# A hybrid decoder step: the cross-attention samples' chain in 20 steps per head, and the GLA gate logits as two rounded products

## The chip, the cores and the metric

The kernel runs on one core of one Trainium2 chip. The metric is the device time of one execution in microseconds (us). Five engines work side by side, each through its own queue in order: TensorE (PE in the profile, its weight loads PEld), VectorE (DVE), ScalarE (ACT), GpSimd (POOL) and SyncE (SP), which here does nothing but issue loads.

## The reference

One layer of a hybrid trunk for a prompt of 1024 tokens and a group of 8 single-token samples. One input projection feeds three branches; each is projected, gated and summed, and one output projection follows. Cut to what the change touches:

```
def mixer_layer(x, mem_k, mem_v, S0, pool_hist, pos0, ...):
    proj = rmsnorm(x) @ w_in
    q, k, v, gla_g, a_lr, u, pool_g, xq, xg, merge = split(proj)
    # A: gated linear attention, 4 heads, key 128, value 256, gate rank 16
    z = a_lr @ w_a2 + b_a                       # the gate logits
    log_a = log_sigmoid(z) / 16
    o, S = gla_chunked(q, k, v, log_a, S0)
    # C: cross attention, 4 heads of 256, over 256 memory rows
    s = einsum('bthd,bmhd->bhtm', xq, mem_k) * 256 ** -0.5
    c = einsum('bhtm,bmhd->bthd', softmax(s), mem_v)
```

The prompt attends to a memory that the kernel projects itself, the same for all 1024 tokens. Each of the 8 samples has memory keys and values of its own (cache_mem_k, cache_mem_v: 256 rows of 256 per head and sample), so its scores are 256 dot products of 256 numbers per head.

## The kernel before

**The projection is the beat.** Products in f32 accuracy are made of rounded halves (type fp32r): each operand is split into hi and lo, and mm3 (L242 to L244) sums hi·hi, hi·lo and lo·hi. The input projection goes by a seven-product scheme (run_product) over 40 column pairs. A product has two stretches of 12 matmuls of 258 columns. Behind each stretch fill() takes the next pieces of a second stream, mix(), by costs that the pieces yield; so between two stretches of the projection stand one or two small pieces of attention. One stretch is called a slot below. mix() runs cross_steps() and then gla_steps(); the first fills about 120 to 370 us of the span, the second the part up to some 700 us.

**What sets the order.** The rows of TensorE and SyncE stand in the order in which the program is written (manual_schedule). VectorE, ScalarE and GpSimd get theirs from a scheduler, which ranks rows by its own estimate. All five then work in order: a row that waits holds everything behind it on its engine. Tiles come from rings: R (14 buffers of 128x512), V (4, loads of keys, values and broadcast queries), W (halves of the projection's weights), and PZ (2 PSUM buffers, for all of attention). A tile can be written only when the last reader of the tile that had its buffer is done.

**Cross attention of the prompt** goes in 16 units s (4 heads by 4 groups of 256 queries). scores(s) (cross_scores, 12 matmuls, L242 to L244) takes keys mkTh and mkTl, and queries xqsh and xq, which cross_queries (L697) splits from a loaded xq on ACT (L226) and DVE (L227). The softmax is on DVE and ACT (nm L709, p L75). weights(s) transposes p (L724) and splits the result into pTh (ACT L223) and pTl (DVE L224). values(s) multiplies them by the memory's values; ACT writes xo (L736), and POOL stores it (L737, mixsc). memory(s) transposes the keys of the next head.

**The samples' chain** (cross_sample, L754) is run one step at a time between these pieces. cross_rows (L744) transposes the scaled queries of the 8 samples to rows, and POOL stores them (L752, tile xqs). fetch(b2) issues, for two samples, two loads of keys (kc, 256 KB each) and one load qb of the two query rows (L767), which repeats each over 128 partitions. DVE multiplies and sums (L777, 4 rows for two samples), into the scores sc. After four pairs: transposes of sc (L791), softmax (nm L793, ps L75, L797, L798), transposes of ps (L803), a copy to pm (L804); then twice four loads vc and 16 matmuls with pm (L817), read by ACT into cs (L819); then transposes of cs (L827). kc, qb and vc share ring V of 4 buffers: a pair's kc and qb take three.

**The gate logits.** w_a2 stays resident as w2, f32, in four copies of its 16 rows at partitions 0, 32, 64 and 96; the projection leaves a_lr as four partial sums at the same partitions, stored in al_scr. gla_load (L896) loads alc, 256 tokens of it, and gla_gates (L904) makes the logits of a head in one f32 matmul (L907), 16 blocks in all; gla_sample does the same for the 8 samples (L1012, 4 blocks).

## Time and profile before

| | us |
|---|---|
| median of 3 runs (lowest, highest) | 1442.38 (1441.68, 1443.36) |
| the profiled execution: its own time | 1445.01 |
| the profiled execution: its span | 1443.3 |
| TensorE busy (share) | 1417.4 (98%) |
| VectorE busy | 916.2 (63%) |
| ScalarE busy | 679.0 (47%) |
| GpSimd busy | 222.1 (15%) |

The profiler records one execution. Its span runs from the first to the last instruction; what lies around it is 1.7 us. An engine's busy time is the time in which it had an instruction at work; matmuls overlap, so a busy TensorE is not one at its peak. The views read below list what an engine waited for and which tile or transfer ended the wait, the busy time of all engines in chosen stretches with the clock granted to TensorE (1.00 is 2.4 GHz, 0.50 is 1.2 GHz), and timelines of single instructions.

### The profile page before, as it was taken

The numbers are of one execution on the slowest core, as the hardware profiler recorded it, in microseconds if no ns is written. First come the engines' busy times: TensorE is split into PE (matmuls) and PEld (weight loads), VectorE is DVE, ScalarE is ACT, GpSimd is POOL, SyncE is SP. The second block draws the span as 40 slices with busy tenths as digits, with TensorE's granted clock in tenths as the row PEclk, the third lists the DMA queues.
The fourth block names the chain that finished last, engine by engine and source line by source line (L and its number), as shares of the span: only waits on it lengthen the run. The fifth ranks groups of instructions, "written<-read, shape, count | busy, mean of one in ns | idle before, by whom it ended". The sixth has DMA issues, their size and how long they took to land.

```text
span 1443.3 us, 28179 instructions
## 1 busy us (share of the span) xinstructions
PE 1417.4 (98%) x10689; PEld 1356.1 (94%) x10689; DVE 916.2 (63%) x2123; ACT 679.0 (47%) x1575; POOL 222.1 (15%) x401
## 2 busy tenths in 40 slices
PE   8999999999999999999999999999999999999998
PEld 6899999989899999999999999999999999999876
DVE  6954756666687777767766778785672434554436
ACT  6743544443465666656654445444472432233212
POOL 3211111124342121212221111111010000000000
PEclk9999999999999999999999999999999999999999
DMA  9355665656656363554654455454694777632633
GB/s 329 125 165 169 217 218 187 207 175 165 198 155 193 115 192 129 182 176 126 187 167 150 149 188 170 159 184 163 204 298 134 234 257 249 234 104 79 224 118 116
DMA packets 183507, 259.42 MB, mean 180 GB/s; under 512 B 22204, under 2 KB 132564, under 8 KB 183364
## 3 DMA queue, kind: packets, MB, share of 16 engines
q1 hardware_dynamic: 159900, 183.87, 41.5%
q0 software_dynamic: 23328, 73.56, 14.7%
q8 instruction: 84, 1.38, 0.4%
q14 instruction: 51, 0.42, 0.1%
q10 hardware_dynamic: 144, 0.20, 0.0%
HBM read 180.47 MB, written 77.56 MB: 179 GB/s over the span
## 4 chain that ended last, share of the span: by engine, by line
PE 88%; DMA 5%; DVE 5%; issue 1%; ACT 1%; SPq 0%; POOL 0%; DVEq 0%; ACTq 0%; POOLq 0%
PE px L242 25%; PE px L243 25%; PE px L244 25%; DMA qb<-xqs 3%; PE pz L244 2%; PE pz L243 2%; PE pz L242 2%; DMA raw<-in_w_in_dram 1%; DVE kc L777 1%; PE pz L963 1%; PE pz L404 1%; PE pz L944 1%; PE pz L817 1%; PE pz L946 1%; PE pz L907 0%
## 5 line engine op out<-in xcount | busy, mean ns | idle before, releaser
L244 PE MATMUL px<-bh,wbl 128*128 128x384 f32 (+1 forms) x576 | 184.1, 320 | 0.0
L243 PE MATMUL px<-bl,wbh 128*128 128x384 f32 (+1 forms) x576 | 184.1, 320 | 0.0
L242 PE MATMUL px<-bh,wbh 128*128 128x384 f32 (+1 forms) x576 | 183.7, 319 | 0.0
L554 ACT ACTIVATE r<-px 128x258 f32<-128x258 f32 x240 | 89.9, 375 | 47.4 <-PE px L244 46.9
L242 PEld LDWEIGHTS px<-bh,wbh 128*128 128x128 f32 x576 | 108.3, 188 | 0.0
L243 PEld LDWEIGHTS px<-bl,wbh 128*128 128x128 f32 x576 | 108.2, 188 | 0.0
L244 PEld LDWEIGHTS px<-bh,wbl 128*128 128x128 f32 x576 | 108.2, 188 | 0.0
L242 PE MATMUL px<-ot,s1h 128*128 128x258 f32 x320 | 94.1, 294 | 0.0
L242 PE MATMUL px<-o,a12h 128*128 128x258 f32 x320 | 93.4, 292 | 0.0
L242 PE MATMUL px<-ot,s3h 128*128 128x258 f32 x320 | 93.2, 291 | 0.0
L242 PE MATMUL px<-o,s4h 128*128 128x258 f32 x320 | 93.0, 291 | 0.2 <-DVE c L636 0.2
L242 PE MATMUL px<-o,a11h 128*128 128x258 f32 x320 | 92.8, 290 | 0.0
L242 PE MATMUL px<-ot,a22h 128*128 128x258 f32 x320 | 92.6, 289 | 0.0
L242 PE MATMUL px<-ot,s2h 128*128 128x258 f32 x320 | 92.2, 288 | 0.0
L243 PE MATMUL px<-o,a11h 128*128 128x258 f32 x320 | 91.1, 285 | 0.3 <-DVE o L224 0.3
L243 PE MATMUL px<-o,a12h 128*128 128x258 f32 x320 | 91.1, 285 | 0.0
L244 PE MATMUL px<-o,a12l 128*128 128x258 f32 x320 | 91.0, 284 | 0.0
L244 PE MATMUL px<-ot,s1l 128*128 128x258 f32 x320 | 90.9, 284 | 0.0
L243 PE MATMUL px<-ot,s1h 128*128 128x258 f32 x320 | 90.8, 284 | 0.0
L244 PE MATMUL px<-o,a11l 128*128 128x258 f32 x320 | 90.6, 283 | 0.0
L243 PE MATMUL px<-ot,s2h 128*128 128x258 f32 x320 | 90.1, 281 | 0.5 <-DVE ot L224 0.5
L243 PE MATMUL px<-ot,a22h 128*128 128x258 f32 x320 | 90.5, 283 | 0.0
(471 smaller groups left out, 4634.3 us busy)
## 6 DMA issues: line engine op xcount, KB each, us to landing
raw<-in_w_in_dram SPq DMA_DIRECT2D x80, 512.0 KB, 4.0
msc<-c POOLq DMA_DIRECT2D x24, 516.0 KB, 4.8
brsc<-c POOLq DMA_DIRECT2D x24, 516.0 KB, 3.7
sig<-msc SPq DMA_DIRECT2D x24, 516.0 KB, 6.0
brr<-brsc SPq DMA_DIRECT2D x48, 256.0 KB, 5.2
wbr<-in_w_branch_dram SPq DMA_DIRECT2D x24, 512.0 KB, 5.5
acc<-sig POOLq DMA_DIRECT2D x16, 516.0 KB, 5.2
acc<-acc SPq DMA_DIRECT2D x16, 516.0 KB, 7.0
```

The lines of the kernel that those rows point to most:

```text
L242: nc.tensor.matmul(out, lhsT=lh, rhs=rh, start=start, stop=False, skip_group_check=more)
L243: nc.tensor.matmul(out, lhsT=lh, rhs=rl, start=False, stop=False, skip_group_check=more)
L244: nc.tensor.matmul(out, lhsT=ll, rhs=rh, start=False, stop=stop, skip_group_check=more)
L404: nc.tensor.matmul(t[:, :DV], lhsT=memT[k // 2][:, k % 2, a * P:(a + 1) * P], rhs=raw[k // 2][:, k % 2], start=k == 0, stop=k == NK - 1)
L554: nc.scalar.activation(r, acc[c][:, :QT], AF.Copy)
L777: nc.vector.tensor_tensor_reduce(kc[:, a, :], kc[:, a, :], qb[:, bb, :], scale=1.0, scalar=0.0, op0=ALU.mult, op1=ALU.add, accum_out=sc[:, ...
L817: nc.tensor.matmul(t[32 * j:32 * j + 32, :DV], lhsT=pm[:, a, 4 * i + j, :], rhs=vc[j][:, a, :], start=a == 0, stop=a == 1)
L944: nc.tensor.matmul(t[0:64, 0:P], lhsT=ki[:, 0:64], rhs=qi, start=True, stop=True)
L946: nc.tensor.transpose(t[:, P:2 * P], kt, ident)
L963: nc.tensor.matmul(to, lhsT=kiqi[:, 1, cs], rhs=st, start=False, stop=True)
```

## The change

**The samples' chain.** Its steps are cut and spread anew, 20 per head instead of 16. One sample's sums are a step of their own. The loads of keys and query rows move to cross_keys, which is called two pairs ahead: for pairs 0 and 1 at the end of the head before, for pairs 2 and 3 at samples 2 and 4. The query rows leave ring V: each sample has a tile qb of its own, in buffers of the tags alc and st, which GLA uses later, and one load of 128 KB; so 32 loads instead of 16. Ring V now holds two pairs of kc. cross_scaled and cross_rows of the next head move behind the softmax and between the two blocks of sample values. There are more steps between the softmax and the transposes of ps, and the loads of vc are issued ahead of these. At the beginning the queries are loaded before the memory's transposes, a step lies between these and the split of the queries, and the rows of head 0 are made right before the first scores.

**The gate logits.** w2 is no longer resident. gate_weights (at unit 6) loads w_a2 eight times into 128 partitions, splits it on ACT and DVE, and stores both halves by eight POOL stores in w2_scr. gate_inputs (at units 7 and 8) loads the stored a_lr, whose 16 rows now stand twice in each group of 32 partitions (wa is copied once more by POOL at the start), and makes of it a stack in which one copy holds the rounded part and the other the rest: one ACT row and two POOL rows of 128x512, and a POOL store. gla_gates then takes two fp32r matmuls, with the halves of w_a2, on the stacked tile. gla_load has one more small load per head.

```
-    w2 = cp.tile([P, 512], F32, name="w2")
-    nc.vector.memset(w2, 0.0)
+    gm = cp.tile([P, 4], F32, name="gm")
+    nc.vector.tensor_reduce(gm[:, 0:2], ident.rearrange("p (j e r) -> p e j r", j=4, e=2), axis=AX.XY, op=ALU.add)
+    nc.vector.tensor_tensor(gm[:, 2:3], gm[:, 0:1], gm[:, 1:2], op=ALU.subtract)
+    second_copy, copy_sign = gm[:, 1:2], gm[:, 2:3]
...
     wa = R([NK, 32], name="wa")
-    nc.vector.memset(wa, 0.0)
 
     def small_loads():
         nc.gpsimd.dma_start(out=wa[:, :, :GATE], in_=w_in[:, O_A:O_A + GATE].rearrange("(k p) n -> p k n", p=P))
-        for j in range(4):
-            nc.gpsimd.dma_start(out=w2[32 * j:32 * j + GATE], in_=w_a2)
+        nc.gpsimd.tensor_copy(wa[:, :, GATE:], wa[:, :, :GATE])
...
+    def cross_keys(h, b2):
+        kc = [loaded(ck[2 * b2 + bb, :, h, :].rearrange("(a p) d -> p a d", p=P), [2, DV], "kc", V) for bb in range(2)]
+        qb = [wk.tile([P, DV], F32, tag=t, name="qb", bufs=2) for t in ("alc", "st")]
+        for bb in range(2):
+            nc.sync.dma_start(out=qb[bb], in_=xq_scr[h][2 * b2 + bb].partition_broadcast(P))
+        cross["kc", h, b2] = kc, qb
+
     def cross_sample(h):
 
-        if h == 0:
-            cross_scaled(0)
-            cross_rows(0)
-            yield 1.2
-            yield 0.5
-            yield 0.5
         sc = wk.tile([P, 16], F32, tag="sc", name="sc", bufs=2)
-
-        def fetch(b2):
-            kc = [loaded(ck[2 * b2 + bb, :, h, :].rearrange("(a p) d -> p a d", p=P), [2, DV], "kc", V) for bb in range(2)]
-            qb = V([2, DV], name="qb")
-            nc.sync.dma_start(out=qb, in_=xq_scr[h][2 * b2:2 * b2 + 2].partition_broadcast(P))
-            return kc, qb
-
-        kcs, qb = fetch(0)
-        yield 0.5
-        yield 0.5
-        for b2 in range(4):
-            for bb in range(2):
-                b, kc = 2 * b2 + bb, kcs[bb]
-                for a in range(2):
-                    nc.vector.tensor_tensor_reduce(kc[:, a, :], kc[:, a, :], qb[:, bb, :],
-                                                   scale=1.0, scalar=0.0, op0=ALU.mult, op1=ALU.add,
-                                                   accum_out=sc[:, a * NS + b:a * NS + b + 1])
-            if b2 == 2 and h + 1 < NH:
-                cross_scaled(h + 1)
-            if b2 < 3:
-                kcs, qb = fetch(b2 + 1)
-                yield 1.2
-            elif h + 1 < NH:
-                cross_rows(h + 1)
-            yield 1
+        for b in range(NS):
+            kcs, qb = cross["kc", h, b // 2]
+            kc = kcs[b % 2]
+            for a in range(2):
+                nc.vector.tensor_tensor_reduce(kc[:, a, :], kc[:, a, :], qb[b % 2],
+                                               scale=1.0, scalar=0.0, op0=ALU.mult, op1=ALU.add,
+                                               accum_out=sc[:, a * NS + b:a * NS + b + 1])
+            if b in (2, 4):
+                cross_keys(h, b // 2 + 1)
+            yield 0.7
...
         nc.vector.tensor_scalar(p, p, sm, None, op0=ALU.mult)
-        yield 1.2
-        yield 0.5
+
+        def own_values(i):
+            return [loaded(cv[4 * i + j, :, h, :].rearrange("(a p) d -> p a d", p=P), [2, DV], "vc", V) for j in range(4)]
+
+        vc = own_values(0)
+        if h + 1 < NH:
+            cross_scaled(h + 1)
+        yield 1.5
         t = PZ()
         for a in range(2):
             nc.tensor.transpose(t[:, a * NS:(a + 1) * NS], p[:, a * P:(a + 1) * P], ident[:NS, :NS])
         nc.vector.tensor_copy(pm[:, :, :, 0], t[:, :2 * NS].rearrange("p (a b) -> p a b", a=2))
-
-        def own_values(i):
-            return [loaded(cv[4 * i + j, :, h, :].rearrange("(a p) d -> p a d", p=P), [2, DV], "vc", V) for j in range(4)]
-
-        vc = own_values(0)
         yield 1.2
         yield 0.5
         cs = R([2, DV], name="cs")
@@ -817,10 +807,20 @@
                     nc.tensor.matmul(t[32 * j:32 * j + 32, :DV], lhsT=pm[:, a, 4 * i + j, :], rhs=vc[j][:, a, :],
                                      start=a == 0, stop=a == 1)
             nc.scalar.activation(cs[:, i], t[:, :DV], AF.Copy)
-            vc = own_values(1) if i == 0 else None
-            yield 1.2
-            yield 0.5
-            yield 0.5
+            if i == 0:
+                vc = own_values(1)
+                yield 2.2
+                yield 0.5
+                if h + 1 < NH:
+                    cross_rows(h + 1)
+                yield 1.2
+                yield 0.5
+        if h + 1 < NH:
+            cross_keys(h + 1, 0)
+        yield 2.2
+        if h + 1 < NH:
+            cross_keys(h + 1, 1)
+        yield 0.5
         t = PZ()
         for i in range(2):
             for d in range(2):
@@ -828,6 +828,7 @@
         for d in range(2):
             nc.vector.tensor_copy(perm8(brs[2][:, 2 * h + d]), column0(t, d))
         yield 1.2
+        yield 0.5
 
     def cross_steps():
...
         samples = chain_of(cross_sample(h) for h in range(NH))
         cross_load(0)
+        cross_fetch(0, 0)
+        cross_fetch(0, 1)
+        yield 1.5
         cross_memory(0)
-        cross_fetch(0, 0)
-        yield 2
         cross_queries(0, 0)
-        cross_fetch(0, 1)
+        yield 1.5
+        cross_scaled(0)
+        cross_rows(0)
+        yield 1
         for s in range(16 + 2):
             if s < 16:
                 scores(s)
+                if s == 0:
+                    cross_queries(0, 1)
                 yield 3
-                if s + 1 < 16:
+                if 0 < s < 15:
                     cross_queries(*divmod(s + 1, 4))
                 if s + 2 < 16:
                     cross_fetch(*divmod(s + 2, 4))
+            if s == 6:
+                gate_weights()
+            elif s in (7, 8):
+                gate_inputs(s - 7)
             if s % 4 == 2 and s < 14:
                 cross_load(s // 4 + 1)
+            if s == 0:
+                cross_keys(0, 0)
+                cross_keys(0, 1)
             if s >= 1:
                 yield next(samples, 0)
             if 0 <= s - 2:
...
+    def gate_weights():
+        w = R([NH, P], name="w2")
+        for j in range(8):
+            nc.gpsimd.dma_start(out=w[16 * j:16 * j + GATE], in_=w_a2.rearrange("r (h n) -> r h n", h=NH))
+        hi, lo = split_in(w, [NH, P], "w2")
+        for j, x in enumerate((hi, lo)):
+            for h in range(NH):
+                nc.gpsimd.dma_start(out=w2_scr[h][:, j], in_=x[:, h].bitcast(F32))
+
+    def gate_inputs(i):
+        def stacked(hi, x):
+            nc.scalar.activation(hi, x, AF.Copy, scale=copy_sign)
+            nc.gpsimd.tensor_scalar(x, x, second_copy, None, op0=ALU.mult)
+            nc.gpsimd.tensor_tensor(hi, hi.bitcast(F32), x, op=ALU.add)
+
+        if i == 0:
+            stacked(als_parts, als)
+        hi = R([512], F32R, "al")
+        stacked(hi, loaded(al_scr[i][:, :512], [512], "alr"))
+        nc.gpsimd.dma_start(out=alp_scr[i], in_=hi.bitcast(F32))
+
     def gla_load(h, c):
-        alc = wk.tile([P, CT], F32, tag="alc", name="alc", bufs=2)
-        nc.sync.dma_start(out=alc, in_=al_scr[c // 2][:, (c % 2) * CT:(c % 2 + 1) * CT])
+        if c == 0:
+            wg = gla["w2", h] = wk.tile([P, 2, P], F32R, tag="w2s", name="w2s", bufs=2)
+            nc.sync.dma_start(out=wg.bitcast(F32), in_=w2_scr[h])
+        alc = wk.tile([P, CT], F32R, tag="alc", name="alc", bufs=2)
+        nc.sync.dma_start(out=alc.bitcast(F32), in_=alp_scr[c // 2][:, (c % 2) * CT:(c % 2 + 1) * CT])
         kq = R([2, CT], name="kq")
         for j, scr in enumerate((k_scr, q_scr)):
             nc.sync.dma_start(out=kq[:, j], in_=scr[h // 2][:, 2 * (h % 2) + c // 2, (c % 2) * CT:(c % 2 + 1) * CT])
@@ -904,7 +942,8 @@
     def gla_gates(h, c):
         alc, kq = gla["in", h, c]
         t = PZ()
-        nc.tensor.matmul(t[:, :CT], lhsT=w2[:, h * P:(h + 1) * P], rhs=alc, start=True, stop=True)
+        for j in range(2):
+            nc.tensor.matmul(t[:, :CT], lhsT=gla["w2", h][:, j], rhs=alc, start=j == 0, stop=j == 1)
         bz = R([2, CT], name="bz")
         b, z = bz[:, 0], bz[:, 1]
         gate_exps(t[:, :CT], CT, h, z, b)
@@ -1009,7 +1048,8 @@
             gla_rows(0)
             yield 1
         t = PZ()
-        nc.tensor.matmul(t[:, :NS], lhsT=w2[:, h * P:(h + 1) * P], rhs=als, start=True, stop=True)
+        for j in range(2):
+            nc.tensor.matmul(t[:, :NS], lhsT=gla["w2", h][:, j], rhs=als_parts, start=j == 0, stop=j == 1)
```

In the order of the instructions the change shows at three places. First, SyncE's queue at the first head's keys; before:

```order
L670 DMA kc_1681<-in_cache_mem_k_dram 128x2x256
L670 DMA kc_1683<-in_cache_mem_k_dram 128x2x256
L767 DMA qb_1685<-xqs0_124 128x512
L296 DMA raw_1691<-in_w_in_dram 128x4x256
L670 DMA xq_1770<-xqsc1_171 128x2x256
L670 DMA mkv_1772<-mkvs01_149 128x512
L670 DMA mkv_1774<-mkvs11_153 128x512
L670 DMA kc_1780<-in_cache_mem_k_dram 128x2x256
L670 DMA kc_1782<-in_cache_mem_k_dram 128x2x256
L767 DMA qb_1784<-xqs0_124 128x512
```

and now:

```order
L673 DMA kc_1603<-in_cache_mem_k_dram 128x2x256
L673 DMA kc_1605<-in_cache_mem_k_dram 128x2x256
L761 DMA qb_1607<-xqs0_126 128x256
L761 DMA qb_1608<-xqs0_126 128x256
L673 DMA kc_1611<-in_cache_mem_k_dram 128x2x256
L673 DMA kc_1613<-in_cache_mem_k_dram 128x2x256
L761 DMA qb_1615<-xqs0_126 128x256
L761 DMA qb_1616<-xqs0_126 128x256
L673 DMA xq_1677<-xqsc0_178 128x2x256
L299 DMA raw_1709<-in_w_in_dram 128x4x256
L673 DMA kc_1728<-in_cache_mem_k_dram 128x2x256
```

Before, a pair's loads stand behind those of the next prompt unit and of the weights (raw), and pair by pair behind the sums that free ring V; now two pairs' loads stand together, ahead of those.

Second, ScalarE's queue about half way through the second head (xo_2634 and xo_2736 are the readers of the prompt values of the same unit; w2h is the split of w_a2, the r, s and a tiles belong to the projection); before:

```order
L736 ACTIVATE xo_2634<-pz_2635 128x512
L655 ACTIVATE c2_2598<-px_2140 128x258
L223 ACTIVATE s3h_2703<-ws_2701 128x512
L655 ACTIVATE c2_2598<-px_2141 128x258
L223 ACTIVATE pTh_2697<-pz_2692 128x512
L223 ACTIVATE a11h_2748<-raw_2477 128x512
L554 ACTIVATE r2_2764<-px_2531 128x258
L75 ACTIVATE p_2781,sm_2782<-pz_2766,nm_2779 128x256 x2
```

and now:

```order
L228 ACTIVATE s3h_2754<-ws_2752 128x512
L228 ACTIVATE a11h_2802<-raw_2491 128x512
L557 ACTIVATE r2_2818<-px_2555 128x258
L228 ACTIVATE w2h_2704<-w2_2695 128x512
L739 ACTIVATE xo_2736<-pz_2737 128x512
L228 ACTIVATE pTh_2783<-pz_2778 128x512
L228 ACTIVATE s4h_2877<-ws_2608 128x512
```

xo stood ahead of s3h, a11h and r2; it now stands behind r2, which reads a finished stretch of the projection, and behind w2h. Behind xo stand pTh and s4h, a half of the weights of the next product but one, whose rest s4l stands on VectorE ahead of pTl.

Third, ScalarE's queue in the middle of the cross part, at the same product of the projection, where a block of the second head's sample values is read into cs (the first block before, the second now); before:

```order
L554 ACTIVATE r2_3163<-px_2920 128x258
L819 ACTIVATE cs_3165<-pz_3166 128x256
L223 ACTIVATE s4h_3199<-ws_2971 128x512
L554 ACTIVATE r2_3196<-px_2921 128x258
L75 ACTIVATE p_3232,sm_3233<-pz_3217,nm_3230 128x256 x2
```

and now:

```order
L557 ACTIVATE r2_3230<-px_2996 128x258
L921 ACTIVATE al_3178<-alr_3179,gm_115 128x512
L809 ACTIVATE cs_3057<-pz_3232 128x256
L228 ACTIVATE s4h_3274<-ws_3037 128x512
L739 ACTIVATE xo_3198<-pz_3199 128x512
L557 ACTIVATE r2_3262<-px_2997 128x258
```

Between r2 and cs there is now al, which waits for the load alr; xo of a prompt unit stands behind both, and takes the buffer of alr when POOL's two rows have read it.

## Rows read from the trace of the kernel before

**Rows 1.** The page, part 1: busy time of each engine (share) x instructions.
```profile
PE 1417.4 (98%) x10689; PEld 1356.1 (94%) x10689; DVE 916.2 (63%) x2123; ACT 679.0 (47%) x1575; POOL 222.1 (15%) x401
```

**Rows 2.** Windows by stage: PE, PEld, DVE, ACT, POOL busy (x), clock, DMA, GB/s.
```profile
120.00:200.00 80.00, 76.47 (x629) 73.46 (x629) 49.38 (x122) 35.80 (x89) 8.99 (x16) 0.98 0.57 174
...
280.00:380.00 100.00, 93.08 (x785) 88.59 (x784) 61.00 (x158) 41.13 (x98) 31.74 (x53) 0.98 0.64 187
```

**Rows 3.** What TensorE waited for, 115 to 372 us: total, times, longest.
```profile
PE pz L803 <- DVE ps L798: 2.4, 1, 2.4
PE pz L243 <- DVE pTl L224: 1.5, 1, 1.5
PE pz L242 <- ACT xqsh L226: 1.4, 1, 1.4
PE pz L244 <- DVE xq L227: 1.2, 2, 0.9
PE pz L724 <- ACT xo L736: 1.1, 1, 1.1
PE pz L817 <- DVE pm L804: 1.0, 1, 1.0
PE pz L791 <- DVE mkTl L224: 1.0, 1, 1.0
PE pz L242 <- DVE pTl L224: 1.0, 1, 1.0
```

**Rows 4.** One 2 us window inside the first cross stretch, same columns as rows 2.
```profile
126.00:128.00 2.00, 2.00 (x12) 2.00 (x11) 0.41 (x2) 1.27 (x5) 0.00 (x0) 0.52 0.99 372
```

**Rows 5.** TensorE timeline at the first scores: start, duration, operation, [idle before <-releaser].
```profile
120.90 0.28 PE L244 MATMUL px<-ot,a22l 128*128 128x258 f32 x1
122.57 0.38 PE L242 MATMUL pz<-mkTh,xqsh 128*128 128x256 f32 x1 [1.39 <-ACT xqsh L226]
122.79 0.28 PE L243 MATMUL pz<-mkTl,xqsh 128*128 128x256 f32 x1
...
124.55 0.42 PE L244 MATMUL pz<-mkTh,xq 128*128 128x256 f32 x1
...
127.78 0.35 PE L244 MATMUL px<-o,a12l 128*128 128x258 f32 x1
```

**Rows 6.** What VectorE waited for, 115 to 385 us: total, times, longest.
```profile
DVE kc L777 <- DMA qb<-xqs: 24.2, 11, 4.1
```

**Rows 7.** Tile qb: time from the issue of its loads to landing.
```profile
DMA to landing us min/median/max: 3.1/4.5/5.6
```

**Rows 8.** VectorE timeline around one late key sum, last head.
```profile
355.06 0.42 DVE L777 CUSTOM_DVE_ANT_0 kc<-kc,qb 128x256 f32<-128x256 f32 x1 [4.10 <-DMA qb<-xqs]
355.42 0.69 DVE L224 TENSOR_TENSOR pTl<-pz,pTh 128x512 fp32r<-128x512 f32 x1
```

**Rows 9.** TensorE timeline at the first gate logits.
```profile
381.10 0.59 PE L907 MATMUL pz<-alc,w 128*128 128x256 f32 x2
...
381.64 0.28 PE L243 MATMUL px<-o,s4h 128*128 128x258 f32 x1
381.76 0.28 PE L244 MATMUL px<-o,s4l 128*128 128x258 f32 x1
```

**Rows 10.** ScalarE by line and shape, 120 to 380 us: busy, mean ns, idle.
```profile
L554 ACT ACTIVATE r<-px 128x258 f32<-128x258 f32 x53 | 20.0, 378 | 14.7 <-PE px L244 14.6
...
L223 ACT ACTIVATE a12h<-raw 128x512 fp32r<-128x512 f32 x9 | 5.7, 633 | 3.9 <-PE px L243 3.5 <-ACT mvsh L223 0.3
```

**Rows 11.** Tile xq (256 KB each): time from the issue of its loads to landing.
```profile
DMA to landing us min/median/max: 3.2/4.3/6.9
```

**Rows 12.** TensorE timeline: one block of 16 sample-value matmuls.
```profile
308.68 1.07 PE L817 MATMUL pz<-vc,pm 128*32 128x256 f32 x16 [0.98 <-DVE pm L804]
```

**Rows 13.** GpSimd by line and shape, whole span: busy, mean ns, idle.
```profile
L1391 POOL COPY mgs<-zeros 128x128 f32<-128x128 f32 x2 | 3.3, 1654 | 3.8 <-DVE bl L224 3.8
masks.py:199 POOL TENSOR_SCALAR_AFFINE_SELECT ident<-ident 128x128 f32<-128x128 f32 x1 | 0.3, 287 | 0.0
```

More of the change, by code (lines that the diff above doesn't have):

```diff
@@ L195, in trunk_kernel @@
     als = cp.tile([P, NS], F32, name="als")
+    als_parts = cp.tile([P, NS], F32R, name="alsp")
     S_XQ, S_Q, S_K, S_V, S_U = 0, 8, 12, 16, 24
@@ L208, in trunk_kernel @@
     al_scr = scratch(2, "als", (P, HT))
+    alp_scr = scratch(2, "alps", (P, 512))
+    w2_scr = scratch(NH, "w2s", (P, 2, P))
     q_scr, k_scr = (scratch(2, s, PAIR) for s in ("qsc", "ksc"))
```

## The prediction

> **What bounds the kernel now.** I read the page's busy times first: TensorE is at work for 1417.4 of 1443.3 us [rows 1]. So time is gained only where TensorE stands still, where its clock falls, or where it gets less to do. I then read the windows by stage, since the change lies in the cross part (120 to 370 us) and in the gate logits behind it. TensorE is idle for 3.5 us from 120 to 200 and for 6.9 us from 280 to 380 [rows 2], 10.4 together. The list of its waits names what ended them: nine stops, 10.6 us, each behind ScalarE or VectorE, and all at attention pieces (pz) [rows 3].
>
> A stop costs more than its idle time. At the first scores the row before starts at 120.90, the second row behind the stop at 122.79 [rows 5]; without the stop that would be 0.24, at the 0.12 from row to row that rows 9 show. So 1.65 us are lost where 1.39 are listed, 0.26 more. Nine stops: 10.6 + 9 x 0.26 = 12.9 us.
>
> Behind two of them the clock falls. From 124.55 to 127.78 fifteen matmuls start 0.215 apart [rows 5], and the window there shows a granted clock of 0.52 [rows 4], the lower of the two levels. At 0.12 they would take 1.8 instead of 3.2: 1.4 us lost. There is one other such stretch, at 367 us, right behind the 2.4 us stop; 2.8 us together.
>
> So all that the cross part can give is 12.9 + 2.8 = 15.7 us, about 1%.
>
> **The change, part by part.**
>
> *The gate logits.* The f32 block starts at 381.10 and the second row of the projection behind it at 381.64; less one row of 0.12 that is 0.42 us for a block [rows 9]. Two fp32r matmuls of 256 columns take 2 x 0.12 = 0.24, as the first scores' rows of the same shape do. So 0.18 less, 16 times: **-2.9 us**. The bound on the other side is 0, if the two cost what the one did. The four blocks of 8 samples go from one f32 to two short matmuls; I take 0. The loads of w2s and alc stay ahead of their use as alc does now, at no cost.
>
> *The sample chain's loads.* VectorE waits 24.2 us, 11 times, for qb [rows 6], which lands 4.5 us after its issue [rows 7]. What stands behind is seen in the last head: the key sum waits 4.10 us, and pTl, which TensorE wants, comes only then, at 355.42 [rows 8]; that is the 1.5 us stop. The stops for ps (2.4), xo (1.1) and mkTl (1.0) also stand behind key sums or behind projection weights whose load SP had queued behind the keys. With two pairs ahead the loads get three or more slots of 12 x 0.12 = 1.4 us, about their landing. The stops for pm (1.0) and the other pTl (1.0) come from a step put too close and from a buffer whose store was late; the steps are now 4 to 5 slots apart there. All six: 8.0 + 6 x 0.26 = **-9.6 us**.
>
> *The first scores.* Of the stops for xqsh and xq, 2.6 us, I expect half to stay: the split now has one slot (1.4 us) of cover, but ScalarE and VectorE do mkTh, xqsh (0.63 each [rows 10]) and then mkTl and xq (0.69 each, as in rows 8) one after the other, 2 us and more. **-1.2 us**.
>
> *New stops.* The order of the rows shows three places where TensorE is left without cover.
> (a) The transposes of sc in the second head wait for PZ, which xo frees; xo is queued on ScalarE behind r2 of the stretch that has just ended, and behind w2h: 0.38 + 0.63 + 0.63 = 1.6 us [rows 10].
> (b) The scores a slot later wait for pTl, queued on VectorE behind s4l, whose s4h needs a weight buffer that the same stretch frees: 0.63 + 0.69 + 0.69 = 2.0 us [rows 8, 10].
> (c) The second alr is loaded into a buffer that the prompt values free. From there to the weights' transposes TensorE has a stretch, 16 sample-value matmuls (1.0 [rows 12]) and a stretch, 3.9 us; the load takes 4.3, with bounds of 3.2 and 6.9 by xq, of equal size [rows 11], then al 0.63 and cs 0.38, queued behind it, 5.3 in all: 1.4 us, with 0.3 and 4.0 as bounds.
> With 0.26 each: **+5.8 us**. They could be smaller if earlier rows run late anyway; none at all is the bound below.
>
> *The clock.* The stretch at 367 goes with its stop. (a) and (b) stand within 4 us of each other, as the stops for xqsh and xq at the first scores did, so I expect one there; the old first one I expect to go with half of its stop: two become one. **-1.4 us**; bounds 0 and -2.8.
>
> *GpSimd and SyncE.* POOL gets 17 rows, 16 of them transfers and small work that its 15% of busy time [rows 1] covers. What matters is the two rows of 128x512 for each alr, since xo of a prompt unit takes alr's buffer. If (c) costs 1.4, xo is wanted 3.9 + 1.4 + 2.9 = 8.2 us after the values, al is done after 4.9, and xo takes 0.6: the two POOL rows have 2.7 us. Nothing here shows such a row. The nearest, AFFINE_SELECT of 128x128, takes 0.287; four times that is 1.15, and the pair 2.3, an estimate: no cost. The other end is COPY of 128x128 with 1.65 [rows 13], four times that 6.6, the pair 13.2. I take the low end, that of the row which, like the new ones, computes in place. The idle time ahead of the COPY ends with a VectorE split (bl), so it ran among those, and part of its 1.65 may be a wait for them that does not grow with a row's length.
> The Trainium skill has a rule that speaks against this placing (SBUF — State Buffer, Who interferes with whom): a VectorE instruction with two inputs in SBUF and a GpSimd instruction that reads SBUF exclude one another, for whole instructions. The two COPY rows agree with it in kind; no run here shows the new rows, which will also stand among splits. By it each would be held for one split of 0.69: the pair 3.7, 1.0 us late, and the sum 1.0 us worse.
>
> *What I can't see.* Some key sums will still come late (the third head's first pair is issued just ahead of its use, the last head's third behind a load of raw), and stores of w2 and alr hold ring buffers. Mostly there are 2 to 6 slots of slack to TensorE: **+1 us**, bounds 0 and 3.
>
> **Sum:** -2.9 - 9.6 - 1.2 + 5.8 - 1.4 + 1.0 = -8.3 us. The profiled execution took 1445.01 us, 1.7 of them around its span; the median of the runs is 1442.38, so this one lies 2.6 above it. The terms are differences and carry over: 1436.7 for such an execution, **1434 us** for the median.
>
> **The rivals.**
> 1. *New stops eat the gain of the cross part* and the logits alone remain. For it: order is all that sets these stops, and new rows have been put on both queues that end them. Against: the six old ones have causes that are gone. With (c) at 4.0, late keys at 3 and no gain from the clock: 1434 + 2.6 + 2 + 1.4 = 1440; within 0.2% from 1439.5 on (2.9 us, about what a measurement of this kernel can tell from no change).
> 2. *Slower: the POOL pair is slow.* At 13.2 us it is 10.5 late for xo behind the second alr. The first alr holds mvsh, a later row of ScalarE, in the same way, with 8 us of room, so 5.2 late: 1434 + 15.7 = 1450. It decides from 8.3 + 2.9 = (p - 2.7) + (p - 8) on, so p = 11 us, 5.5 for a row. For it: the COPY rows. Against: the AFFINE_SELECT row, of the same size, at a sixth of that.
> 3. *All stops go*, the scheduler's new rows included, and both stretches of low clock: 1442.4 - 2.9 - 12.9 - 2.8 = 1424. For it: that the steps are farther apart everywhere. Against: (a) and (b) follow from the rows' order and from buffers alone.
> 4. *The logits give nothing*: 1437. The change would not do what it says there.
>
> **How the numbers follow.** My forecast, with (a) to (c) more or less as costed, 1428 to 1438: 0.48. Logits without gain, 1437: 0.07. Rival 1, up to 1445: 0.25, of which 0.14 are within 0.2% of before and 0.11 still faster. Rival 3: 0.09. Rival 2 and its like, above 1445.3: 0.11. Faster: 0.48 + 0.07 + 0.11 + 0.09 = 0.75; same 0.14; slower 0.11. The range of 8 in 10 leaves out most of rival 3 and the top: 1427 to 1443.
>
> **What would show it.** The gate block on TensorE should fall from 0.42 to about 0.24. The waits of VectorE for qb should fall from 24 to some 10 us. TensorE's list should lose ps, pm, xo and both pTl of rows 3, keep a shorter xqsh, and show three new stops, at sc's transposes, at scores and at p's transposes, between 195 and 230 us. I am wrong if those three are absent, if a POOL row of 128x512 takes over 2 us, or if a low clock shows in two or more places of the cross part.

## The result: slower by a quarter of a per cent

The changed kernel takes 1446.1 us (median of 19 runs) where the kernel before takes 1442.7 (19 runs beside them). The ratio is 1.0024, with a 95% interval from 1.0016 to 1.0033. The forecast was 1434, faster, with a range up to 1443. The profiled execution of the changed kernel took 1446.0 us, with a span of 1444.2. That of before was one of its longer ones (1445.0), so the two spans lie only 0.9 us apart; the forecast for such an execution was 1436.7, so 9.3 us have to be found. Against the medians the miss is 12.1; the other 2.8 are in the carrying over, since this execution of before lay 2.3 above its kernel's median, and that of the changed kernel lay on it. An execution's time goes with its granted clock: of 23 executions of before, timed beside the run of the chain alone below, the six at 0.996 took 1444.5 us in the mean and the five at 0.999 took 1441.4; all 19 of the changed kernel lie between 0.994 and 0.997.

The page after, part 1, answers to [rows 1]: TensorE has 2.6 us less work, about what the logits were to save, and the kernel is no faster.

```profile
span 1444.2 us, 28278 instructions
...
PE 1414.8 (98%) x10689; PEld 1354.7 (94%) x10689; DVE 912.9 (63%) x2124; ACT 679.3 (47%) x1579; POOL 244.6 (17%) x422
```

The windows by stage, after (TensorE alone: us, busy, granted clock, DMA share, GB/s), beside [rows 2]:

```profile
120.00:200.00 80.00, 78.32 (x663) 1.00 0.62 193
200.00:280.00 80.00, 68.65 (x542) 0.94 0.66 208
280.00:380.00 100.00, 100.00 (x862) 1.00 0.62 185
```

Both stages in which the kernel before lost time are mended: idle falls from 3.5 to 1.7 us and from 6.9 to 0, with the full clock. But from 200 to 280, where before was never idle, 11.35 us are lost now, and the clock falls. The list of TensorE's waits after (total, times, longest) says to what:

```profile
PE pz L247 <- DVE pTl L229: 6.8, 2, 4.5
...
PE pz L780 <- ACT xo L739: 2.0, 1, 2.0
PE pz L1103 <- ACT os L1097: 1.4, 1, 1.4
PE pz L727 <- ACT p L75: 1.2, 1, 1.2
PE px L247 <- DVE c L648: 0.8, 1, 0.8
```

Of [rows 3] the stops for ps, xo ahead of p's transposes, pm, mkTl and both old pTl are gone, and those for xqsh and xq are short (0.3 and 0.7). The new ones stand within 56 us; TensorE's timeline after gives their places:

```profile
207.64 0.39 PE L247 MATMUL px<-o,a12h 128*128 128x258 f32 x1 [0.83 <-DVE c L648]
...
210.58 0.66 PE L727 MATMUL pz<-ident,p 128*128 128x128 f32 x4 [1.22 <-ACT p L75]
...
216.10 0.42 PE L780 MATMUL pz<-ident,sc 128*8 128x128 f32 x2 [1.96 <-ACT xo L739]
...
223.57 0.55 PE L247 MATMUL pz<-mkTh,xqsh 128*128 128x256 f32 x1 [4.47 <-DVE pTl L229]
...
255.27 0.66 PE L727 MATMUL pz<-ident,p 128*128 128x128 f32 x4 [0.37 <-ACT cs L809]
...
263.40 0.39 PE L247 MATMUL pz<-mkTh,xqsh 128*128 128x256 f32 x1 [2.28 <-DVE pTl L229]
```

**A ruler for the parts.** The view of one line gives the start of its first and last row. Taken for the gate logits, it cuts the span in three: all that the chain and the preparation of the stacked inputs do lies before the first block, what the two products save lies between first and last. Before, then after:

```profile
L907 PE MATMUL pz<-alc,w x32: 377/378/382, 381.1 to 699.1; 128*128 128x256 f32 x32
```
```profile
L946 PE MATMUL pz<-alc,w2s x32: 274/282/366, 383.8 to 698.6; 128*128 128x256 f32 x32
```

The first block comes 2.7 us later (forecast: 5.4 earlier). From first to last it takes 314.8 instead of 318.0, 3.2 less (forecast: 2.9). From there to the end it takes 745.6 instead of 744.2, 1.4 more (forecast: 0), as much as the new stop for os. 2.7 - 3.2 + 1.4 = +0.9, the difference of the spans.

**What ended the new stops.** VectorE's rows ahead of the two longest, after:

```profile
219.65 0.69 DVE L229 TENSOR_TENSOR s4l<-ws,s4h 128x512 fp32r<-128x512 f32 x1 [2.48 <-ACT s4h L228]
222.74 0.69 DVE L229 TENSOR_TENSOR pTl<-pz,pTh 128x512 fp32r<-128x512 f32 x1 [2.40 <-DMA w2s<-w2h]
...
262.66 0.69 DVE L229 TENSOR_TENSOR pTl<-pz,pTh 128x512 fp32r<-128x512 f32 x1 [3.69 <-DMA alps<-al]
```

Both times pTl is held not by a row but by a store: it takes the ring buffer of w2h, then that of al, and such a buffer is free only when the store that reads it has landed. GpSimd's rows show when the stores left:

```profile
215.85 2.14 POOL L917 DMA_DIRECT2D w2s<-w2h  x4 [2.86 <-ACT w2h L228]
217.98 2.12 POOL L917 DMA_DIRECT2D w2s<-w  x4
...
232.44 1.57 POOL L922 TENSOR_SCALAR alr<-alr,gm 128x512 f32<-128x512 f32 x1 [9.49 <-ACT al L921]
234.10 1.28 POOL L923 TENSOR_TENSOR al<-al,alr 128x512 fp32r<-128x512 f32 x1
```

The view of tile w2s, for GpSimd's rows alone, names all who waited for these eight stores, and their time from issue to landing:

```profile
who waited for it (us, times):
  ACT ps L75: 3.7, 1
  DVE pTl L229: 2.4, 1
  POOL mixsc L740: 2.2, 1
...
DMA to landing us min/median/max: 3.9/5.0/5.9
```

Behind the stops of 1.96, of 4.47 and of 2.28 the clock is at the lower of its two levels; windows of 2 us of the changed kernel show it:

```profile
218.00:220.00 2.00, 1.10 (x6) 0.57 1.04 366
...
224.00:226.00 2.00, 2.00 (x11) 0.50 0.12 41
...
264.00:266.00 2.00, 2.00 (x12) 0.52 0.19 27
```

**The second head's keys.** SyncE's rows after: the second head's last two pairs of keys and queries are issued late, behind a load of raw that had waited for its buffer, and then eight in a row.

```profile
196.11 0.38 SPq L299 DMA_DIRECT2D raw<-in_w_in_dram  x1
196.59 0.53 SPq L673 DMA_DIRECT2D xq<-xqsc  x1
197.17 1.31 SPq L673 DMA_DIRECT2D kc<-in_cache_mem_k_dram  x2
198.53 1.51 SPq L761 DMA_DIRECT2D qb<-xqs  x2
200.09 1.40 SPq L673 DMA_DIRECT2D kc<-in_cache_mem_k_dram  x2
201.53 1.48 SPq L761 DMA_DIRECT2D qb<-xqs  x2
```

The first qb of these came to VectorE at 205.87, after 7.1 us of waiting, the longest of ten such waits (17.4 us in all; 24.2 in [rows 6]). TensorE's stops for c and p, at 207.64 and 210.58, come right behind it.

### The profile page after: what moved, and what is told of

It is laid out like the page before. It is cut to its first block, busy times and chain, and to the rows that moved or that the text cites. A ratio compares the mean times of both kernels' runs of the same rounds, so it can differ in the third digit from the quotient of the medians.

```text
span 1444.2 us, 28278 instructions
## 1 busy us (share of the span) xinstructions
PE 1414.8 (98%) x10689; PEld 1354.7 (94%) x10689; DVE 912.9 (63%) x2124; ACT 679.3 (47%) x1579; POOL 244.6 (17%) x422
## 4 chain that ended last, share of the span: by engine, by line
PE 90%; DVE 4%; DMA 3%; ACT 1%; issue 1%; POOL 0%; DVEq 0%; SPq 0%; ACTq 0%; POOLq 0%
PE px L247 26%; PE px L248 25%; PE px L249 25%; PE pz L247 3%; PE pz L249 2%; PE pz L248 2%; DMA raw<-in_w_in_dram 1%; PE pz L407 1%; PE pz L1002 1%; PE pz L983 1%; PE pz L985 1%; PE pz L807 0%; DVE ws L308 0%; PE pz L727 0%; DMA qb<-xqs 0%
## 5 line engine op out<-in xcount | busy, mean ns | idle before, releaser
L247 PE MATMUL px<-ot,s3h 128*128 128x258 f32 x320 | 93.3, 292 | 0.0
L247 PE MATMUL px<-ot,s1h 128*128 128x258 f32 x320 | 93.0, 291 | 0.0
L249 PE MATMUL px<-ot,s3l 128*128 128x258 f32 x320 | 90.8, 284 | 0.0
L248 PE MATMUL px<-ot,s3h 128*128 128x258 f32 x320 | 90.7, 284 | 0.0
L249 PE MATMUL px<-ot,s2l 128*128 128x258 f32 x320 | 90.6, 283 | 0.0
```

The costliest lines, as they stand in the source:

```text
L247: nc.tensor.matmul(out, lhsT=lh, rhs=rh, start=start, stop=False, skip_group_check=more)
L248: nc.tensor.matmul(out, lhsT=lh, rhs=rl, start=False, stop=False, skip_group_check=more)
L249: nc.tensor.matmul(out, lhsT=ll, rhs=rh, start=False, stop=stop, skip_group_check=more)
```

## The experiments

Medians stand with their ratio to the kernel before on the same chip.

### The two halves of the change apart

The chain alone, and the logits alone with their preparation among the pieces of the old chain. Edits, against the kernel before, in words:

```
+ chain: 20 steps, cross_queries in V tiles, splits as after;  logits as before
```
```
+ logits: gate_weights, gate_inputs, two products as after;    chain as before
```

> The change's samples' chain alone, gate logits as before. Theory A (the changed kernel's loss from 200 to 280 us comes from the gate pieces: pTl and ps stand in ring buffers of w2h, w2 and al, which are free only when GpSimd's stores of them have landed): the stops of 4.5 and 2.3 us for pTl and the 2.0 us stop at sc's transposes are gone, with the low clock behind them; the gains at 120 to 130 us and 280 to 380 us stay (4 and 9 us); some 1432 us beside 1442 to 1443 of before. Rival B (the new order of steps and the denser loads of keys are what stops TensorE there, whatever the gate pieces do): the idle time from 200 to 280 us stays near 11 us and the time is some 1449, the changed kernel's without the logits' gain.

> The change's gate logits alone, samples' chain as before. Theory A: 2.9 us are gained at the 16 blocks, and more is lost around 200 to 280 us, where tiles of the prompt's attention meet buffers held by GpSimd's stores: 1443 to 1452, so slower than before or the same. Rival B: the gate pieces cost little by themselves, 1440.

Measured: the chain alone 1439.6 us, 0.9976 [0.9966, 0.9986]; the logits alone 1452.8 us, 1.0064 [1.0047, 1.0081]. The gate blocks of the two:

```profile
L914 PE MATMUL pz<-alc,w x32: 377/378/382, 373.1 to 690.9; 128*128 128x256 f32 x32
```
```profile
L939 PE MATMUL pz<-alc,w2s x32: 274/281/364, 394.3 to 709.6; 128*128 128x256 f32 x32
```

So the chain alone gains 8.0 us before the first block. With the logits the first block comes 13.2 us later than before (in the longest of the six executions, 1456.0), on the new chain 10.7 later (383.8 against 373.1): so more than the products save is lost ahead of them, where their preparation stands. Between the blocks both kernels with two products save 2.7 to 3.2 us. The stop for os is in the chain alone too (1.4 us), so it comes with the chain.

### Where the preparation's price lies

First other tiles: w2, w2h, al and alr in ring E instead of R, at the same place.

```
- w = R([NH, P], name="w2")
+ w = E([NH, P], name="w2")
...
- hi = R([512], F32R, "al")
+ hi = E([512], F32R, name="al")
```

> The changed kernel, but w2, w2h, al and alr stand in the ring of long tiles (tag e) instead of ring R; nothing else. Theory A: no pTl or ps waits for a store of w2 or al; the stops of 4.5 and 2.3 us go, and the low clock from 216 to 226 us; what the order of the queues alone costs (xo behind w2h, some 2 us) may stay: 1431 to 1436. Rival B: as the changed kernel, 1446.

Measured: 1442.6 us, 0.9997 [0.9985, 1.0008]. Both stops for pTl are gone, which bears out that the ring's buffers made them, and the first block comes at 378.7, 5.1 us earlier. But E has readers of its own: a tile c of the projection now waits for a gate tile, and TensorE for it.

```profile
PE px L247 <- DVE c L648: 4.0, 2, 2.9
```

Then another place: the same rows in the memory stage, ahead of the cross part.

```
- if s == 6: gate_weights()
- elif s in (7, 8): gate_inputs(s - 7)
+ (slot 23) gate_weights();  (slots 25, 26) gate_inputs(0), gate_inputs(1)
```

> The changed kernel, but gate_weights at slot 23 and gate_inputs at slots 25 and 26, between the memory's projection and the cross part, in place of units 6, 7 and 8; the gate pieces themselves are the same and still use ring R. Theory A (a gate piece costs what its place makes of it: in the cross part tiles of the attention meet its buffers while the stores of GpSimd are under way): the stops for pTl of 4.5 and 2.3 us and for sc's transposes go, the chain's own late keys (some 4.5 us of idle time from 200 to 280 us, as in the run of the chain alone) stay, and the logits' 2.9 us are kept: 1437, 2 to 3 us below the chain alone. Rival B (the stores and the three GpSimd rows cost about the same wherever they stand): 1442 to 1446.

Measured: 1443.6 us, 1.0005 [0.9996, 1.0014]. The stops from 200 to 280 fall to about those of the chain alone (74.07 us busy of 80, against 75.45), and one of 5.3 comes in at 126.56, for mkTl:

```profile
PE pz L247 <- DVE mkTl L229: 5.3, 1, 5.3
```

VectorE stood still there 5.21 us for a small copy of GpSimd's (smp), which was queued behind the four rows for alr and al and the two stores of al.

Then fewer rows, at the first place: one row of VectorE in place of GpSimd's two, two stores in place of eight.

```
- nc.gpsimd.tensor_scalar(x, ...); nc.gpsimd.tensor_tensor(hi, ...)
+ nc.vector.scalar_tensor_tensor(hi, x, second_copy, hi, ...)
...
- for h in range(NH): dma_start(out=w2_scr[h][:, j], in_=x[:, h])
+ dma_start(out=w2_scr[:, j], in_=x)
```

> The changed kernel with the gate pieces at their places, but the stack made by one VectorE row (0.69 us) instead of two on GpSimd (3.0 us), and the halves of w_a2 stored by one transfer each instead of four. Theory A (tiles of the attention wait for GpSimd's rows and stores of the gate pieces): with the buffers held shorter (a store of 0.5 us instead of 2.1, no 3 us of arithmetic), the stops of 4.5 and 2.3 us for pTl shrink to some 2 and 0.5: 1440 to 1443. Rival B (the two GpSimd rows and eight stores don't matter, it is the queues' order): 1445 to 1447.

Measured: 1445.0 us, 1.0013 [1.0003, 1.0023].

```profile
PE pz L247 <- DVE pTl L229: 7.7, 2, 5.4
```

Neither GpSimd's arithmetic nor the number of stores makes these two stops. One store of 256 KB landed 6.5 us after its issue, and pTl waited 5.35 for it; the landing time is their price.

The lean form was also put into the memory stage (slots 15, 17, 19).

> As the run before, and gate_weights at slot 15, gate_inputs at slots 17 and 19, so that all of it is done before the first tile of the cross part. Theory A: none of the gate pieces' stops is left, and what remains is the chain alone less the logits' 2.9 us: 1436 to 1438. Rival B: the logits give nothing by themselves or cost elsewhere, 1440 to 1444.

Measured: 1445.0 us, 1.0017 [1.0005, 1.0029], with a stop of 4.7 for wmsh, the memory projection's weights. It moved again instead of going.

### The late keys

The chain alone, with the loads of keys and queries on GpSimd's queue; first for all heads, then for all but the last.

```
- nc.sync.dma_start(out=kc[bb], ...);  nc.sync.dma_start(out=qb[bb], ...)
+ queue = nc.gpsimd if h < NH - 1 else nc.sync     (first form: nc.gpsimd)
+ queue.dma_start(out=kc[bb], ...);  queue.dma_start(out=qb[bb], ...)
```

> The samples' chain alone (gate logits as before), with the loads of keys and query rows in GpSimd's queue instead of SyncE's. Theory C (the second head's last two pairs come late because SyncE holds a load of raw until 196 us, and the keys' loads stand behind it): VectorE's 7.1 us wait for qb goes, and the four stops from 207 to 227 us, 4 us of idle time; 1435 to 1437 beside 1439.6. Rival D (eight loads at once land late, 6.5 us after their issue, whatever the queue): no change, 1439 to 1441, or worse if GpSimd's loads hold up its stores of xo.

> The samples' chain alone, keys and query rows of the first three heads in GpSimd's queue, those of the last in SyncE's. Theory C: both the stops from 207 to 227 us and the one at 340 us, which came where GpSimd was busy with stores of v, are gone: 1435 to 1437. Rival D: some other stop comes in their place, 1439 to 1442.

Measured: for all heads 1441.3 us, 0.9985 [0.9976, 0.9994]; for all but the last 1435.8, 0.9944 [0.9932, 0.9956]. In the first form the last head's keys stood behind eight stores of vtsc (5.2 us on GpSimd, up to 328.6), and a stop of 4.2 came in for sc's transposes. The six sums right ahead of it ran one after the other from 337.84, behind other rows of VectorE, and none waited for a load; so the trace shows VectorE's order there, and not how much the stores did. In the second form the window that lost 4.55 us in the chain alone is full:

```profile
200.00:280.00 80.00, 80.00 (x683) 1.00 0.68 213
```

The second head's last two pairs now left GpSimd from 189.32 to 194.37, where SyncE, held by raw, had issued them from 197.34 to 202.66; the longest wait for qb fell from 7.1 to 1.4. So SyncE's order, raw first, made the late keys. They also landed sooner: in the stretch from 180 to 215 us qb took 3.7 to 4.5 us, where the chain alone had 5.4 to 6.4, and no run takes the two apart. Both mendings at once, keys for all heads on GpSimd's queue and the preparation at slots 23 to 26, added up their two new stops:

> The changed kernel with both: gate pieces at slots 23, 25 and 26, and the loads of keys and query rows in GpSimd's queue. Theories A and C: 1432 to 1435, faster than before by 0.5% and more. Rivals B and D: 1442 to 1447.

Measured: 1444.3 us, 1.0015 [1.0005, 1.0026].

### Do the two products pay at all?

The mended chain (keys as in the second form) with the lean preparation in the memory stage:

```
+ queue = nc.gpsimd if h < NH - 1 else nc.sync
+ (slots 15, 17, 19) lean gate_weights(), gate_inputs(0), gate_inputs(1)
```

> The two runs before in one kernel. If A and C hold and add up: 1432 to 1435, 0.6% below before. If either fails: 1437 or more.

Measured: 1438.6 us, 0.9964 [0.9952, 0.9976], slower than the mended chain alone (1435.8).

```profile
PE pz L247 <- ACT wmsh L228: 5.2, 1, 5.2
```

On ScalarE wmsh stood behind w2h, which waited 3.43 us for the load of w; seven of these eight loads had been queued on GpSimd behind eight stores of mkv.

Next, halves of 256 columns, still in the memory stage, in the idle buffers of qb and w2s, each load well ahead; beside it the mended chain alone once more.

```
+ GATE_LOADS = {3: 0, 4: 1, 14: 2, 15: 3, 18: 4, 21: 5}
+ GATE_PARTS = {10: 0, 13: 1, 17: 2, 19: 3, 22: 4, 25: 5}
...
```

> Chain of the change with its keys on GpSimd's queue for all heads but the last (as in the run of the chain alone so done), and the two-product logits prepared in the memory stage, in halves of 256 columns, in tiles that nothing else uses at that time (those of qb and of w2s), each load some 8 us or more ahead of its split; VectorE writes the second half in one row, no GpSimd arithmetic. Theory A (the two products do save their 2.9 us on TensorE, and all that the change lost with them was where their preparation stood): the 5.2 us stop for wmsh and every stop behind gate tiles are absent, the cross part is as in the run of the chain alone, and the gate blocks save 2.9 us more: about 1433, 0.2% below the chain alone run beside it. Theory B (the two products give nothing, or the new loads, the f32r tiles or the samples' blocks give it back in the GLA stage): the same as the chain alone, 1436. Theory C (the preparation costs wherever it stands): 1438 to 1441, with a new stop in the memory stage.

> The chain alone with its keys on GpSimd's queue for all heads but the last, on the same chip as the run with the logits: 1436, as before; the difference of the two is what the logits' two products are worth. Theory A: this one is 2.9 us slower than the other. Theory B: no difference. Theory C: this one is 2 to 5 us faster.

Measured: with the logits 1437.4 us, 0.9961 [0.9948, 0.9973]; without them 1434.8, 0.9948 [0.9931, 0.9964]. The intervals overlap, but no gain of 2.9 shows. The ruler tells why, with the logits and without:

```profile
L954 PE MATMUL pz<-alc,w2s x32: 274/281/364, 376.3 to 691.1; 128*128 128x256 f32 x32
```
```profile
L917 PE MATMUL pz<-alc,w x32: 377/377/382, 368.5 to 686.3; 128*128 128x256 f32 x32
```

3.0 us are saved between the blocks, and 7.8 lost before them. So the products do save, and the preparation eats it. To be sure of it, the preparation was left out, first on the changed kernel's own chain, then on the mended one. The logits are then not the reference's; the products, the sizes of the GLA stage's loads and the small stack of the 8 samples stay:

```
- gate_weights();  al's split, load and store in gate_inputs
+ gla_load reads al_scr for both operands
```

> The changed kernel as it is, with the two products for the logits, but without the preparation of their stacked inputs: the weights' split, the split of al and their loads and stores through scratch are left out, and the two products read al's first version instead (so the gates are not the reference's; the loads in the GLA stage are of the same sizes). What is disputed is whether the logits' saving is real and only its preparation costs. Theory A (yes): first to last gate block 315 us as in the changed kernel, before it as in the chain alone, so 3 us below the chain alone: 1436.5, and the preparation where it stands costs 9 to 10 us. Theory B (the saving is given back somewhere behind, to the longer loads or to the clock): as the chain alone, 1439.5, and the preparation costs 6.5.

> The same without preparation, with the keys on GpSimd's queue for all heads but the last. Theory A: 3 us below the chain alone so done (1434.8 to 1435.8 in two runs): 1432.3, and so the preparation moved to the memory stage costs some 5 us. Theory B: 1435.3, and it costs 2.

Measured: 1437.2 us, 0.9963 [0.9948, 0.9977], and 1432.4 us, 0.9923 [0.9907, 0.9938]. The blocks of the first, then of the second:

```profile
L932 PE MATMUL pz<-alc,w2s x32: 274/282/366, 373.3 to 688.1; 128*128 128x256 f32 x32
```
```profile
L932 PE MATMUL pz<-alc,w2s x32: 274/282/366, 368.4 to 683.2; 128*128 128x256 f32 x32
```

Theory A holds: without the preparation the changed kernel is 9 us faster (1446.1 to 1437.2), and the first block comes 10.5 us earlier. The list of waits of this kernel has no stop for pTl, and that for xo is down to 0.7; from 100 to 500 us no window of it shows the lower clock.

### A version that beats both

All of the preparation again, in the same halves, but one piece in every second step of the chain, in the two buffers of w2s that stand empty until the GLA stage. Each piece is placed behind the splits of weights and activations that stand ahead of it (issue_after), all its loads are on GpSimd's queue, and VectorE makes the stack in one row, as in the lean form.

```
+ if s < 12:
+     with tc.issue_after(last["hi"].ins), tc.issue_after(last["lo"].ins):
+         (gate_parts if s % 2 else gate_load)((2, 3, 4, 5, 0, 1)[s // 2])
...
```

> The changed kernel's chain with the keys on GpSimd's queue for all heads but the last, and the full preparation of the logits' inputs, but in six pieces of 256 columns, one in every second step of the chain, in the two buffers of w2s that nothing uses before the GLA stage; each load a whole step of the chain ahead of its split, each store a step ahead of the next load. If the preparation cost what it did because its tiles and queues were shared and its loads and stores too close (the theory that the runs have borne out so far), it costs at most 1 us of its rows here, and the kernel comes near the one without preparation (1432.4 in the run before this): 1432.5 to 1433.5, gate blocks from 366 to 369 us on. If preparing costs wherever it stands, by its rows on ScalarE, VectorE and GpSimd's queue alone: 1436 to 1438, with new stops between 125 and 280 us.

Measured: 1432.1 us, 0.9923 [0.9908, 0.9939], as fast as the kernel without preparation.

```profile
L954 PE MATMUL pz<-alc,w2s x32: 274/280/363, 369.3 to 684.0; 128*128 128x256 f32 x32
```

The first block is 0.9 us later than without preparation, one execution of each. So in this form the preparation costs about 1 us, and against the mended chain alone (1434.8 and 1435.8, on other chips) the two products now gain some 3. Shared buffers, with stores and loads close to their use, explain the rest as far as the stops for pTl show it; this run changes place, buffers, distances and the lean row at once, and does not say what each is worth.

## Why the prediction was wrong

By the ruler the forecast before the first block was -9.6 - 1.2 - 2.8 for old stops and old clock, +1.0 for what could not be seen, +5.8 for new stops and +1.4 for the clock behind them: -5.4. The runs give each group apart.

- **The old stops and the old clock: right.** The mended chain without preparation has its first block at 368.4, 12.7 earlier than before (others of the mended chain at 368.5 and 369.9); forecast 13.6. This holds against the profiled execution of before, with both its low stretches: the chain alone gains 6.2 us of span on that one, but 3.6 in the medians.
- **"What I can't see": the term that was mis-sized.** Forecast +1.0 (0 to 3), measured 4.9 (373.3 against 368.4). The prediction named the third head's first pair and, behind raw, the last head's third, and took it that most have slack. It was the second head, behind raw, and not one pair but two, eight loads in a row. The waits for qb, which were to fall from 24 to some 10 us, fell to 17.4.
- **New stops (a) to (c): the step that failed.** Forecast with their clock 7.2, measured 10.5 (383.8 against 373.3). The places of (a) and (b) were right, the price was not: slack was counted in rows of engines. (b) was s4l and pTl one after the other, 2.0 us; it took 4.47, since pTl got w2h's buffer and its stores, issued from 215.85 on, had not landed. Less the 2.40 that VectorE waited for them it is 2.07, the forecast's own sum. Without preparation (b) is not there at all. (c) was the load of the second alr ahead of p's transposes, 1.4 us. There 0.37 were lost; 2.28 were lost eight microseconds later, by the store of al, issued at 258.63, for which pTl waited until 262.66. The prediction said that stores of w2 and alr hold ring buffers, and put that under slack instead of following each buffer to its next tile. The new stops also stand where the late keys' stops stood: those for p at the scores, ps and c take 4.6 us without preparation and 1.6 with it.
- **(a): right in kind.** 1.96 against 1.6: on ScalarE r, w2h and xo follow one another from 214.67 to 216.05. Without w2h 0.7 remain.
- **The clock: the term was too small, and its sign of being wrong came true.** Two old low stretches were to become one, 1.4 us. Three came, one behind each long new stop: 11 rows from 216.53 to 218.69, 13 from 223.92 to 226.49 and 16 from 264.10 to 267.31. Their 37 steps of about 0.215 us would be 0.12 at the full clock: 3.5 us, 2.1 more than forecast. The prediction named a low clock in two or more places as a sign that it is wrong. The profiled execution without preparation has none in the cross part, so here all of it comes with the new stops.
- **The logits: right.** 3.2 against 2.9. TensorE's timeline after, at the first block: from its start to that of the next row there are 0.24 us, as forecast, where [rows 9] gave 0.42.

```profile
383.85 0.40 PE L946 MATMUL pz<-alc,w2s 128*128 128x256 f32 x2
384.09 0.29 PE L247 MATMUL px<-o,s4h 128*128 128x258 f32 x1
```

- **GpSimd's pair: close.** Forecast 2.3, with 2.7 as the point from which it costs; measured 1.57 + 1.28 the first time and 1.57 + 1.63 the second, 2.9 and 3.2. A longer pair delays the store of al by as much, but the lean form without it was no better. By the rule of the Trainium skill (SBUF — State Buffer, Who interferes with whom) the pair was to take 3.7, the prediction's estimate; the trace lies between the two. It agrees in kind for TENSOR_TENSOR, on both sides: GpSimd's second one, which met a VectorE row that ran to 257.18, took 1.63 instead of 1.28; and a split that met the first (234.10 to 235.38) took 1.18 where splits take 0.69. In the run of the logits alone two such VectorE rows took 2.18 and 2.06. A split that met TENSOR_SCALAR, at 255.77, took 0.69 as ever.

```profile
234.75 1.18 DVE L229 TENSOR_TENSOR a12l<-raw,a12h 128x512 fp32r<-128x512 f32 x1 [2.56 <-ACT a12h L228]
```

- **The tail.** The stop for os, 1.4 us, came with the chain. The traces show where it comes from: TensorE's sample matmuls ahead of it start at 741.02 instead of 742.93, about one slot earlier in the order, while ScalarE has os ready only 0.4 us earlier (747.87 against 748.30). What moved these matmuls no run here tested; it stays open.

Rival 1 (new stops eat the gain, up to 1445) was the right mechanism, and its top was 1 us short: it held late keys to 3 and (c) to 4.0, counted no gain from the clock where 0.7 more than before were lost (3.5 against 2.8), and had no longer end for (b). Rival 2's price, a slow pair, was not it.

In sum: 0.9 (old terms) + 3.9 (keys) + 1.2 (new stops) + 2.1 (their clock) - 0.3 (logits) + 1.4 (os) = 9.2 of the 9.3 us that had to be found.

## What to carry to other kernels

A store from a shared buffer is a user of that buffer until it has landed. So follow each new tile to the tile that takes its buffer next, and put the store's landing, here 4 to 6.5 us, into the slack; rows of engines alone give too small a price. Price the clock with a stop: here 2 to 3 us of rows at half the clock stood behind each of the three long ones. Work that has time is best spread, one piece to a step, in buffers that stand empty, with each load a step ahead of its row. And where a change has two halves, look for a row that divides the span between them: its first and last start size each half without any run.

## What the runs showed of the hardware

- The eight stores of 64 KB of w2h and w landed 3.9 to 5.9 us after issue, and a single one of 256 KB, in the lean form, after 6.5. The Trainium skill (DMA: Bandwidth & Descriptors, Anatomy of one DMA) says that a transfer's semaphore is raised only once its last byte is confirmed landed, with about 2 us fixed; the trace agrees in kind, as pTl started only then, and its times are two to three times that.
- qb landed 3.0/5.5/7.6 us after issue (least, median, most) against 3.1/4.5/5.6 in [rows 7]. Its loads are half as large and twice as many now, and often eight loads stand in a row; which of it makes the difference no run shows. On GpSimd's queue, also eight in a row, they took 3.7 to 4.5.
- A GpSimd row of 128x512 f32 takes 1.57 us (with a scalar) and 1.28 to 1.63 (of two tiles), 4.5 to 5.7 times the 0.287 of [rows 13], a row of a quarter of the size. Three VectorE rows with two inputs that met the row of two tiles took 1.18, 2.06 and 2.18 us instead of 0.69.
